# A two-layer diffusion step on one core: other homes for split weights, token-ordered output products, and new step lengths in the planner

## The chip, the cores and the metric

The kernel runs on one core of a Trainium2 chip. The metric is the device time of one execution in microseconds, from start to end on that core; smaller is better. A core has five engines that run side by side, each its own stream of instructions in order: TensorE (PE; its weight loads are shown apart as PEld), VectorE (DVE), ScalarE (ACT), GpSimd (POOL) and SyncE (SP), which here only issues DMA transfers.

## The reference: what is computed

One inference step of a two-layer backbone, for one prompt of 128 tokens and 256 latent tokens (384 tokens, three tiles of 128), model width 1024. Every number is fp32. The core of a layer, cut from the reference:

```python
sh1, sc1, g1, sh2, sc2, g2 = jnp.split(mod, 6, axis=-1)      # mod = silu(c) @ w_mod + b_mod
h = rmsnorm(x, p['norm1_g']) * (1 + sc1) + sh1
proj = h @ p['w_in']
q_r, f_f, f_b, i_r, g_r, q_a, k_a, v_a = jnp.split(proj, ...)
...
o_r = o_f + o_b[:, ::-1]                                     # 4 recurrent heads, both directions
o_r = rmsnorm(o_r, p['hgrn_norm_g']).reshape(B, T, W_R) * jax.nn.silu(g_r)
...
o_a = attend_blocks(qa, k_all, v_all)                        # 8 query heads on 2 key heads
x = x + g1 * (jnp.concatenate([o_r, o_a], axis=-1) @ p['w_out'])
h2 = rmsnorm(x, p['norm2_g']) * (1 + sc2) + sh2
x = x + g2 * (jnp.square(jax.nn.relu(h2 @ p['w1'])) @ p['w2'])
```

After two layers comes a last rmsnorm with a gain. Outputs are both token groups' results, the prompt's new keys and values of each layer, and the final states of the recurrent scan.

## The kernel before

**Split weights.** Matmuls run on operands of a reduced fp32 format, so each fp32 operand is split into a hi half and a lo half, and each product is three matmuls added up in one PSUM bank: hi·hi, lo·hi, hi·lo. A weight block (128 x 1024, or 128 x 768 for the query and key rows) is loaded by SP into one of four `raw` buffers; ACT copies it to the hi half (`hi_chain`, L403); DVE subtracts to the lo half (`lo_chain`, L411), which frees the raw buffer. A half is freed by the last matmul that reads it. There are four ordinary `hi` and four ordinary `lo` buffers. Some blocks are marked in a table `extra` with a class of their own and take their halves from memory that is idle at that time: in before, class "C" (a third of the MLP weights, in region C) and class "U" (see below).

**Regions.** Three large areas of SBUF have several lives. A and B (5376 columns each) hold the recurrent scan's data of one pair of heads each, and afterwards the MLP: columns 0 to 3071 hold the hi (A, `mA`) and lo (B, `mB`) halves of the MLP's input, and columns from 3072 on the halves of its activations. C holds token data and later "C" weights. `Hh` and `Hl` (8 blocks of 384 columns) hold the halves of the normalised layer input; when the input projection is done, blocks 0 to 3 take the recurrent heads' outputs.

**A layer.** Normalise the input and transpose it (L521 square, L524 scale and bias of the mean, L537 scale, L542 transposes, L554/556 modulation, L565/566 split). Query/key rows, eight blocks `qk` k = 0 to 7, three tiles, each with a 512-column (L618) and a 256-column matmul (L619). Feature tiles of the scan (L637). Chunks i and g, the values and gates (L596). Between these stand attention (L824, L846, L892) and the scan of the two pairs of heads: levels (L991), the two 64-level pieces (L977), state (L1060, L1066), then for each pair of heads and token tile the head output, three matmuls (L1089, L1092, L1093). Its way on is a chain over four engines: ACT squares (L1101), DVE (L512) and POOL (L514, a power) make the reciprocal root, DVE scales and gates (L1108, which reads the gate product of that tile), PE transposes (L1113), ACT (L1117) and DVE (L1118) split the result into `Hh` and `Hl`. Then the output projection, 48 steps of three matmuls (L668): step (j, t, hf) multiplies tile t by half hf of the columns of weight block j; j = 0 to 3 are the attention blocks `outA`, j = 4 to 7 the recurrent ones `outR` 0 to 3, where 4 and 5 need the first pair of heads and 6 and 7 the second. DVE updates x (L696 times the gate row G, L698 add). Norm again, then the MLP: first product (L1179, with L1194 for its head part), activation (ACT L1164/1166, DVE L1167), second product (L1205), x update. After the second layer: gain multiply (DVE L1267), norm, scale (L1255/1257), output DMA (L1261). Modulation weights are multiplied by c either on PE (L458, two rows of output only) or on DVE (L427), between other work.

**What sets the order.** The order of instructions is made when the program is built, by a list scheduler (`Sched`). The work is written as chains that yield steps: engine, estimated length, what it reads and writes, which buffers it takes and gives back, and for PE a kind (d dense products; t transposes, m and f other small matmuls) and a `hold`. The scheduler keeps a clock per engine, works out when each chain's next step could start, and picks the one with the smallest value, adjusted by priority; what it picks is emitted, and every engine gets its instructions in that order. So a longer estimate for one step moves others. For PE the value is worked out in `start_of`:

```python
sw = self.SWITCH.get((self.kind, kind), 0.0)
v = max(s + hold, free) if self.kind == "d" else max(s, free) + (STAY if kind == "d" else 0.0)
```

`s` is when its data are there, `free` when PE is. After a dense step, a small one is valued as if its data came `hold` (1 or 2 us) later; after a small step, in before, another small one counts from the moment its data are there, and a dense one 0.15 later.

**Names and lines that the change touches.** `units` is the order in which weights are loaded; `wcls` gives a block's class; `hi_chain` waits for the region of a class to be ready; `win_chain`, `wout_chain` are the products of the input and output projection; `mlp_reg` hands out regions A and B for the MLP; `hg_reg` hands them to the scan; `mlp_chain` is the MLP on PE; `final_gain` is L1267.

## Time and profile before

| | |
|---|---|
| median of 3 runs | 988.65 us |
| lowest, highest | 988.31, 991.17 us |
| the profiled execution | 988.47 us |
| its span | 986.7 us |
| mean granted TensorE clock | 0.998 |
| busy: PE / PE weight load | 98% / 85% |
| busy: DVE / ACT / POOL | 69% / 51% / 4% |
| HBM over the span | 166 GB/s |

The span runs from the first to the last instruction that the profiler recorded; the profiled execution took 1.77 us more than its span. A busy share is that of the whole span. In lists of waits, a line such as "PE bank L1113 <- DVE t L1108: 1.4, 6, 0.4" says that PE, at line 1113, writing a PSUM bank, was idle for what DVE wrote at line 1108: 1.4 us in total, in 6 places, 0.4 the longest. A line of the timeline gives the start in us, the duration, engine, line, operation, output and inputs, the matmul's size, output shape, how many were put together (x8), and in brackets the idle time just before with what ended it. Buffer numbers are left out of names: `t` is one of eight scratch tiles, `bank` one of eight PSUM banks, `cst` the constants with the identity, `sm` small statistics.

### The profile page before, as it was taken

Reading aid. Unit: us, or ns where it says so; the run is one execution under the profiler, and the core shown is the slowest. Engines: PE = TensorE matmul, PEld = TensorE weight load, DVE = VectorE, ACT = ScalarE, POOL = GpSimd, SP = SyncE. Lnnn points to the kernel's source line nnn. Section 1 sums busy time; section 2 is a strip of 40 time slices with the busy share of each in tenths; the row PEclk is TensorE's granted clock in tenths of the full one; section 3 lists DMA queues with packets and bytes.
Section 4 is the critical chain, followed back from the end, with each engine's and each line's share of the span. In section 5 each row is a group of like instructions: output and inputs, shape, how many; then the busy total and the mean of one; then the engine's idle time right before and its main releaser. Section 6 shows DMA issues by size and latency. Waiting matters only on the chain.

```text
span 986.7 us, 17386 instructions
## 1 busy us (share of the span) xinstructions
PE 971.8 (98%) x6935; PEld 837.2 (85%) x6937; DVE 684.9 (69%) x1180; ACT 499.7 (51%) x913; POOL 36.0 (4%) x37
## 2 busy tenths in 40 slices
PE   8999999999999999999999999999999999999997
PEld 5796788878989889889888879787899999999895
DVE  3688777777788989989575979967765444444436
ACT  4467564546543444444445686645664444444332
POOL 0020000010000000000001100011100000000000
PEclk9999999999999999999999999999999999999999
DMA  9968676252677787877525322433336444544511
GB/s 312 305 181 253 196 223 189 59 167 88 207 231 249 246 256 236 242 252 233 173 74 144 105 68 87 110 95 112 113 117 217 147 124 149 147 148 149 192 44 64
DMA packets 140801, 165.39 MB, mean 168 GB/s; under 512 B 5889, under 2 KB 105889, under 8 KB 140209
## 3 DMA queue, kind: packets, MB, share of 16 engines
q1 hardware_dynamic: 140720, 164.29, 54.4%
q8 instruction: 54, 0.88, 0.4%
q14 instruction: 27, 0.21, 0.1%
HBM read 161.35 MB, written 2.92 MB: 166 GB/s over the span
## 4 chain that ended last, share of the span: by engine, by line
PE 90%; DMA 4%; DVE 3%; issue 1%; ACT 1%; POOL 1%; SPq 0%; POOLq 0%; ACTq 0%; DVEq 0%
PE bank L1179 26%; PE bank L1205 26%; PE bank L637 9%; PE bank L596 6%; PE bank L668 6%; PE bank L618 3%; PE bank L619 1%; PE bank L892 1%; PE bank L458 1%; PE bank L991 1%; PE bank L846 1%; PE bank L1194 1%; DMA eB<-w_mod_d 1%; PE bank L824 1%; PE bank L542 1%
## 5 line engine op out<-in xcount | busy, mean ns | idle before, releaser
L403 ACT CAST hi<-raw 128x1024 fp32r<-128x1024 f32 (+1 forms) x152 | 155.7, 1029 | 117.5 <-DMA raw<-w_d 45.3
L411 DVE TENSOR_TENSOR lo<-raw,hi 128x1024 fp32r<-128x1024 f32 (+1 forms) x152 | 179.5, 1192 | 50.7 <-ACT hi L403 50.2
L427 DVE SCALAR_TENSOR_TENSOR t<-raw,cT,t 128x512 f32<-128x512 f32 x196 | 135.2, 745 | 8.6 <-DMA raw<-w_mod_d 8.4
L1179 PE MATMUL bank<-mA,hi 128*128 128x384 f32 (+1 forms) x336 | 111.5, 332 | 0.0
L1179 PE MATMUL bank<-mA,lo 128*128 128x384 f32 (+1 forms) x336 | 111.1, 331 | 0.0
L1179 PE MATMUL bank<-mB,hi 128*128 128x384 f32 (+1 forms) x336 | 110.9, 330 | 0.0
L1167 DVE TENSOR_TENSOR mB<-t,mA 128x384 fp32r<-128x384 f32 x64 | 35.7, 557 | 102.7 <-ACT mA L1166 102.5
L1164 ACT ACTIVATE t<-bank 128x384 f32<-128x384 f32 x64 | 31.4, 491 | 140.1 <-PE bank L1179 140.0
L1205 PE MATMUL bank<-lo,mA 128*128 128x512 f32 (+1 forms) x255 | 99.3, 389 | 0.0
L1205 PE MATMUL bank<-hi,mB 128*128 128x512 f32 (+1 forms) x255 | 99.2, 389 | 0.0
L1205 PE MATMUL bank<-hi,mA 128*128 128x512 f32 (+1 forms) x255 | 99.0, 388 | 0.0
L1179 PE MATMUL bank<-mA,wts 128*128 128x384 f32 (+1 forms) x352 | 89.4, 327 | 0.0
L1205 PE MATMUL bank<-wts,mA 128*128 128x512 f32 (+1 forms) x268 | 87.8, 389 | 0.0
L403 ACT CAST wts<-raw 128x1024 fp32r<-128x1024 f32 x44 | 46.2, 1050 | 50.5 <-DMA raw<-w_d 27.2
L411 DVE TENSOR_TENSOR wts<-raw,wts 128x1024 fp32r<-128x1024 f32 x44 | 53.6, 1222 | 21.6 <-ACT wts L403 21.4
L637 PE MATMUL bank<-Hh,hi 128*128 128x384 f32 x192 | 67.7, 352 | 0.0
L1179 PEld LDWEIGHTS bank<-mA,hi 128*128 128x128 f32 x336 | 63.2, 188 | 1.9 <-issue 0.4
L637 PE MATMUL bank<-Hh,lo 128*128 128x384 f32 x192 | 64.6, 336 | 0.0
L637 PE MATMUL bank<-Hl,hi 128*128 128x384 f32 x192 | 64.4, 335 | 0.0
L1179 PEld LDWEIGHTS bank<-mB,hi 128*128 128x128 f32 x336 | 63.2, 188 | 1.4
L1179 PEld LDWEIGHTS bank<-mA,wts 128*128 128x128 f32 x352 | 62.6, 188 | 1.7 <-issue 0.9
L1179 PEld LDWEIGHTS bank<-mA,lo 128*128 128x128 f32 x336 | 63.2, 188 | 0.0
(251 smaller groups left out, 1947.2 us busy)
## 6 DMA issues: line engine op xcount, KB each, us to landing
raw<-w_d SPq DMA_DIRECT2D x128, 512.0 KB, 4.4
raw<-w_mod_d SPq DMA_DIRECT2D x80, 512.0 KB, 3.8
raw<-w_in_d SPq DMA_DIRECT2D x40, 512.0 KB, 4.5
raw<-w_in_d SPq DMA_DIRECT2D x16, 384.0 KB, 6.2
G<-grow SPq DMA_DIRECT2D x4, 1024.0 KB, 5.9
raw<-w_out_d SPq DMA_DIRECT2D x16, 256.0 KB, 3.9
raw<-w_out_d SPq DMA_DIRECT2D x8, 512.0 KB
eB<-w_mod_d SPq DMA_DIRECT2D x12, 256.0 KB, 5.3
```

What stands on the lines that cost most here:

```text
L403: yield S("ACT", c_act(n), lambda u=u, n=n: ACT.copy(out=get(("hi",) + u)[:, 0:n], in_=get(("raw",) + u)[:, 0:n]), r=[("rawk",) + u] + ([( ...
L411: yield S("DVE", c_dve(n), lambda u=u, n=n: V.tensor_tensor(out=get(("lo",) + u)[:, 0:n], in0=get(("raw",) + u)[:, 0:n], in1=get(("hi",) + ...
L427: V.scalar_tensor_tensor(out=o, in0=raw, scalar=c, in1=o, op0=ALU.mult, op1=ALU.add)
L458: PE.matmul(get(nm)[32 * j:32 * j + m, 0:N], cT[:, k, 0:m], raw[:, o:o + N], start=k == 0, stop=k == 7, tile_position=(0, 32 * j))
L596: PE.matmul(ps, a, b, start=(first and k == 0 and i == 0), stop=(last and k == kk - 1 and i == 2))
L618: PE.matmul(get(aq), a, b[:, 0:512], start=st and i == 0, stop=sp and i == 2)
L637: PE.matmul(ps, a, b, start=(k == 0 and i == 0), stop=(k == 7 and i == 2))
L668: PE.matmul(ps, a, b, start=j == 0 and i == 0, stop=j == 7 and i == 2)
L1164: yield S("ACT", c_act(384, True), lambda: ACT.activation(out=get(r_)[:, 0:384], in_=get(z)[:, 0:384], func=AF.Relu), r=[z], acq=[("t2", r ...
L1167: yield S("DVE", c_dve(384), lambda: V.tensor_tensor(out=get(u)[1], in0=get(t_)[:, 0:384], in1=get(u)[0].bitcast(F32), op=ALU.subtract), r ...
L1179: PE.matmul(get(z)[:, cs], a, b, start=(k == 0 and i == 0), stop=(k == 7 and i == 2))
L1205: PE.matmul(get(bank)[:, c0 % 512:c0 % 512 + c1 - c0], a, b, start=(f == f0 and i == 0), stop=(f == NF - 1 and i == 2))
```

## The change

**Homes of split weights.** Of the output projection's recurrent blocks, `outR` 2 and 3 had the class "U" before: columns 3072 to 5119 of regions A and B, ready when both pairs of heads are done. Now `outR` 0 has class "H", the upper four blocks of `Hh` and `Hl`, ready when the last product of the input projection is issued; `outR` 1 has class "A", columns 3072 to 5119 of region A, ready when the first pair of heads is done; 2 and 3 take ordinary buffers. `mlp_reg` hands out A and B in two steps for this. Of the second layer's query/key blocks, k = 0 to 2 have a new class "Q": columns 0 to 3071 of regions A (hi) and B (lo), ready after the last first product of the MLP of layer 0 (`qfree`). The scan of layer 1 then also waits for the last query/key product before it takes the regions.

**Order of the output projection.** The first two weight blocks, j = 0 and 1, are now taken tile by tile (t, hf, j) where before all tiles were done with one block (j, t, hf). The other six were by tiles already.

**The slack rule.** After a small step, another small one is now valued as if its data came up to `SLACK` = 0.5 us later.

**Step lengths.** Ten estimated lengths on DVE and ACT are made longer (by 0.1 to 0.6 us); one line stands for them below. `final_gain` has a later priority (3.0 for 2.125).

```diff
+QN = 3
+SLACK = 0.5
+FG_P = 3.0
...
-        v = max(s + hold, free) if self.kind == "d" else max(s, free) + (STAY if kind == "d" else 0.0)
+        v = max(s + hold, free) if self.kind == "d" else max(s, free) + STAY if kind == "d" else max(s + min(hold, SLACK), free)
...
-        yield S("DVE", 0.6, lb3, r=["lb2"], w=["lb"])
+        yield S("DVE", 1.2, lb3, r=["lb2"], w=["lb"])
...
-                    r=[("rawk",) + u] + ([({"C": "wtsreg", "U": "mlpreg"}[extra[u]], u[0])] if u in extra else []), ...
+                    r=[("rawk",) + u] + ([({"C": "wtsreg", "A": "mlpregA", "H": "hfree", "Q": "qfree"}[extra[u]], u[0])] if u in extra else []), ...
...
-        yield S("PE", 0.0, lambda: None, w=[("win_done", l)])
+        def hfree():
+            for c, t in (("hiH", Hh), ("loH", Hl)):
+                sch.add_slots((c, l), [t[:, 4:8].rearrange("p a b -> p (a b)")[:, 0:1024]])
+        yield S("PE", 0.0, hfree, w=[("win_done", l), ("hfree", l)])
...
-        for j in range(8 - WOT):
-            for t in range(NT):
-                for hf in range(2):
+        for t in range(NT):
+            for hf in range(2):
+                for j in range(8 - WOT):
                     yield step(j, t, hf, (t, hf) == (2, 1))
...
-                r=(["early_done"] if hp else []) if l == 0 else [("mlp_done", l - 1)], w=[("hgreg", l, hp)])
+                r=(["early_done"] if hp else []) if l == 0 else [("mlp_done", l - 1), ("acc", l, "qa", NT - 1, "done")], w=[("hgreg", l, hp)])
...
+        def f0():
+            a = region("A", f"mA{l}", F32R)
+            sch.add_slots(("hiA", l), [a[:, 3072:4096]])
+            sch.add_slots(("loA", l), [a[:, 4096:5120]])
+            mreg[l] = [a]
...
-            for c, r in (("hiU", a), ("loU", b)):
-                sch.add_slots((c, l), [r[:, 3072 + i * 1024:4096 + i * 1024] for i in range(2)])
...
-        yield S("POOL", 0.0, f, acq=[("rA", ("rmA", l)), ("rB", ("rmB", l))], r=[("ot", l, 0), ("ot", l, 1)], w=[("mlpreg", l)])
+        yield S("POOL", 0.0, f0, acq=[("rA", ("rmA", l))], r=[("ot", l, 0)], w=[("mlpregA", l)])
+        yield S("POOL", 0.0, f, acq=[("rB", ("rmB", l))], r=[("ot", l, 0), ("ot", l, 1)], w=[("mlpreg", l)])
...
+        def qfree():
+            for c, r in zip(("hiQ", "loQ"), mreg[l]):
+                sch.add_slots((c, l + 1), [r[:, i * 1024:(i + 1) * 1024] for i in range(QN)])
+        yield S("PE", 0.0, qfree, w=[("qfree", l + 1)])
...
+            extra.update({(l, "qk", k): "Q" for k in range(QN)})
...
-        extra.update({(l, "outR", h): "U" for h in range(8 - WOT, 4)})
+        extra.update({(l, "outR", 0): "H", (l, "outR", 1): "A"})
...
-            sch.spawn(final_gain(t), 2.125)
+            sch.spawn(final_gain(t), FG_P)
```

The changed program has up to 15 lines more: L411 is L414 there, L524 is L527, L537 is L540, L596 is L599, L668 is L674, L696/698 are L702/704, L1089/1092/1093 are L1095/1098/1099, L1113 is L1119, L1267 is L1282.

**DVE at the boundary of the layers.** The rows are DVE's, from the x updates at the end of the first layer's MLP (L696, L698; `x_92` to `x_94` are the three tiles) to the second layer's norm; `lo` buffers filled from `raw` with 768 columns are the second layer's query/key rows. Before, around the first two of these lo halves:

```order
L537 TENSOR_SCALAR t_6_113<-x_93,sm 128x512
L537 TENSOR_SCALAR t_7_114<-x_93,sm 128x512
L698 TENSOR_TENSOR x_94<-x_94,t_3_110 128x512
L554 TENSOR_SCALAR t_0_107<-bank_63,modA_82,modS_86 128x128 x4
L411 TENSOR_TENSOR lo_124<-raw_117,hi_120 128x768
L696 TENSOR_TENSOR t_5_112<-bank_65,G 128x512
L566 TENSOR_TENSOR Hl<-t_4_111,Hh 128x4x128
L566 TENSOR_TENSOR Hl<-t_0_107,Hh 128x4x128
L698 TENSOR_TENSOR x_94<-x_94,t_5_112 128x512
L411 TENSOR_TENSOR lo_125<-raw_115,hi_121 128x768
```

And now:

```order
L414 TENSOR_TENSOR mB_2274<-raw_115,mA_2272 128x768
L702 TENSOR_TENSOR t_1_108<-bank_67,G 128x512
L704 TENSOR_TENSOR x_92<-x_92,t_1_108 128x512
L414 TENSOR_TENSOR mB_2274<-raw_117,mA_2272 128x768
L414 TENSOR_TENSOR mB_2274<-raw_118,mA_2272 128x768
L702 TENSOR_TENSOR t_4_111<-bank_61,G 128x512
L704 TENSOR_TENSOR x_92<-x_92,t_4_111 128x512
L414 TENSOR_TENSOR lo_123<-raw_116,hi_119 128x768
L527 TENSOR_SCALAR sm<-sm 128x1
```

The lo halves of k = 0 to 2 are made in region B (`mB`), around the first tile's x updates and ahead of its norm; that of k = 3 follows in an ordinary buffer. Before, they came behind the second tile's norm, among the third tile's x updates.

**PE at the head outputs of the first layer.** The rows are PE's, from the head outputs of the second pair of heads (three matmuls each; `hg` is the scan's region, `tok` the token data, `S_103` a state) on; two transposes with `cst` are one head pair's output on its way back, L668 (L674) is the output projection, L599 the gate chunk. Before:

```order
L1089 MATMUL bank_68<-tok_539,hg_538 128x128
L1092 MATMUL bank_68<-hg_538 128x128
L1093 MATMUL bank_68<-S_103,hg_538 128x128
L1113 MATMUL bank_62<-cst,t_1_108 128x128 x2
L668 MATMUL bank_61<-hi_119,mAh 128x512
L668 MATMUL bank_61<-hi_119,mAl 128x512
L668 MATMUL bank_61<-lo_123,mAh 128x512
L668 MATMUL bank_64<-hi_119,mAh 128x512
```

And now:

```order
L1095 MATMUL bank_61<-tok_539,hg_538 128x128
L1098 MATMUL bank_61<-hg_538 128x128
L1099 MATMUL bank_61<-S_103,hg_538 128x128
L1119 MATMUL bank_64<-cst,t_6_113 128x128 x2
L599 MATMUL bank_63<-hi_122,Hh 128x512
L599 MATMUL bank_63<-hi_122,Hl 128x512
L599 MATMUL bank_63<-lo_126,Hh 128x512
L599 MATMUL bank_63<-hi_122,Hh 128x512
L599 MATMUL bank_63<-hi_122,Hl 128x512
L599 MATMUL bank_63<-lo_126,Hh 128x512
L1119 MATMUL bank_65<-cst,t_3_110 128x128 x2
L1119 MATMUL bank_67<-cst,t_5_112 128x128 x2
```

The last six products of the gate chunk come behind the head outputs, between two pairs of transposes; before, the gate chunk was done by then, and the output projection's first products followed the transposes.

**DVE at the end.** The rows are DVE's last x updates of the third tile, in quarters (256 columns), with the gain multiply (L1267, in the change L1282) and the first step of the last norm (L524, L527). Before:

```order
L696 TENSOR_TENSOR t_0_107<-bank_66,G 128x256
L1267 TENSOR_TENSOR t_5_112<-x_94,S_103 128x256
L524 TENSOR_SCALAR sm<-sm 128x1
L698 TENSOR_TENSOR x_94<-x_94,t_0_107 128x256
L696 TENSOR_TENSOR t_7_114<-bank_68,G 128x256
L698 TENSOR_TENSOR x_94<-x_94,t_7_114 128x256
L1267 TENSOR_TENSOR t_3_110<-x_94,S_103 128x256
L524 TENSOR_SCALAR sm<-sm 128x1
```

And now:

```order
L702 TENSOR_TENSOR t_0_107<-bank_63,G 128x256
L704 TENSOR_TENSOR x_94<-x_94,t_0_107 128x256
L527 TENSOR_SCALAR sm<-sm 128x1
L702 TENSOR_TENSOR t_7_114<-bank_64,G 128x256
L704 TENSOR_TENSOR x_94<-x_94,t_7_114 128x256
L1282 TENSOR_TENSOR t_5_112<-x_94,S_103 128x256
L1282 TENSOR_TENSOR t_4_111<-x_94,S_103 128x256
L527 TENSOR_SCALAR sm<-sm 128x1
```

The gain multiply that stood between the last two x updates now stands behind both.

More of the change, by code (lines that the diff above doesn't have):

```diff
@@ L262, in ini @@
             V.memset(sel[:, 33:34], 1.0)
-        yield S("DVE", 1.0, ini, w=["ini"])
+        yield S("DVE", 1.25, ini, w=["ini"])
         yield S("ACT", 1.5, lambda: ACT.activation(out=sg, in_=smalls[:, 0:16], func=AF.Sigmoid), r=["smalls"], w=["sg"])
@@ L840, in nrm @@
                 V.tensor_scalar(out=get(pp[kv]), in0=get(pp[kv]), scalar1=mx[:, 4 + kv:5 + kv], scalar2=None, op0=ALU.mult)
-        yield S("DVE", 0.08 + 2 * c_dve(384, True, 1), nrm, r=[nm + (2,)], w=[nm + (3,)])
+        yield S("DVE", 0.2 + 2 * c_dve(384, True, 1), nrm, r=[nm + (2,)], w=[nm + (3,)])
         def tr():
@@ L876, in nrm @@
             V.tensor_tensor(out=v3(get(pp), 4), in0=v3(get(pp), 4), in1=bc(mx[:, 8:12], 128), op=ALU.mult)
-        yield S("DVE", 0.1 + c_dve(512), nrm, r=[pp], w=[pp + (2,)])
+        yield S("DVE", 0.2 + c_dve(512), nrm, r=[pp], w=[pp + (2,)])
         def tr():
@@ L961, in pr @@
             V.tensor_tensor(out=PR[:, cs], in0=PR[:, cs], in1=get(tk)[:, 0:384], op=ALU.mult)
-        yield S("DVE", 2 * c_dve(384), pr, r=[("hgs3", l, h, d) for d in range(2)] if l else [], acq=[("t2", tk)], rel=[tk], w=[("hgi", l, h)])
+        yield S("DVE", 1.05, pr, r=[("hgs3", l, h, d) for d in range(2)] if l else [], acq=[("t2", tk)], rel=[tk], w=[("hgi", l, h)])
     def hg_levels(l, hp):
@@ L1043, in pl32 @@
                 ACT.copy(out=at(j, 32, 32 * (j ^ 1)), in_=v3(get(("hgp", l, hp, 6))[32 * j:32 * j + 32, 0:192], 6))
-        yield S("ACT", 4 * c_act(192, True), pl32, r=[("hgp", l, hp, 7)], rel=[("hgp", l, hp, 6)], w=[("AT", l, hp, 1)])
+        yield S("ACT", 1.15, pl32, r=[("hgp", l, hp, 7)], rel=[("hgp", l, hp, 6)], w=[("AT", l, hp, 1)])
         def pl():
@@ L1048, in pl @@
                 V.tensor_copy(out=at(j, 32, 32 * j), in_=AC[32 * j:32 * j + 32])
-        yield S("DVE", 4 * c_dve(192, True), pl, r=[("hgp", l, hp, 7), ("AC", l, hp)], w=[("AT", l, hp, 2)])
+        yield S("DVE", 0.95, pl, r=[("hgp", l, hp, 7), ("AC", l, hp)], w=[("AT", l, hp, 2)])
     def hg_state(l, h):
@@ L1132, in f @@
             V.tensor_tensor(out=v3(gSs[l][t], 4), in0=v3(gSs[l][t], 4), in1=hg.unsqueeze(1).to_broadcast([128, 4, 128]), op=ALU.mult)
-        yield S("DVE", 2 * c_dve(512), f, r=[("gs", l, t), "consts"], rel=[ag], w=[("gS", l, t)])
+        yield S("DVE", 1.32, f, r=[("gs", l, t), "consts"], rel=[ag], w=[("gS", l, t)])
     mreg = {}
```

10 lines of the change are left out of this document (4 added, 6 removed).

## The prediction

> **What bounds the kernel now.** I read the page first, then the list of TensorE's waits, then the busy time by stage, and last the rows around each wait. On the page: the span, TensorE's busy line and its row of the slices.
>
> ```profile
> span 986.7 us, 17386 instructions
> PE 971.8 (98%) x6935; PEld 837.2 (85%) x6937; DVE 684.9 (69%) x1180; ACT 499.7 (51%) x913; POOL 36.0 (4%) x37
> PE    8999999999999999999999999999999999999997
> ```
>
> PE (TensorE) is busy in 971.8 of 986.7 us; 14.9 us are all that any order of the work can win without removing a matmul, and this change removes none: by the order of instructions both programs issue 5805 matmuls, line by line the same counts. Only the first and the last slice are under nine tenths. So the question is how much of the small idle time in between goes. TensorE's waits, with total, count and longest:
>
> ```profile
> PE bank L311 <- DVE sel L260: 2.1, 1, 2.1
> PE bank L1113 <- DVE t L1108: 1.4, 6, 0.4
> PE bank L458 <- DMA raw<-w_mod_d: 0.7, 1, 0.7
> PE bank L618 <- DVE lo L411: 0.7, 1, 0.7
> PE bank L542 <- DVE t L537: 0.6, 2, 0.4
> PE bank L977 <- ACT hg L1006: 0.5, 1, 0.5
> PE bank L458 <- DMA eB<-w_mod_d: 0.4, 1, 0.4
> PE bank L458 <- DMA eC<-w_mod_d: 0.3, 1, 0.3
> PE bank L458 <- issue: 0.3, 1, 0.3
> ```
>
> They sum to 7.0 us. 2.1 is the first instruction, 1.0 the last three lines (the start), and 3.9 lies in places that the change reorders: six waits at the transposes of the head outputs (L1113), one at a modulation weight (L458), one at the next layer's first rows (L618), part of L542's, and one at the 64-level of the scan (L977). Where nothing waits the stream is full; by stage, with us, then busy us of PE, weight load, DVE, ACT and POOL, then clock:
>
> ```profile
> 190.00:207.00 17.00, 16.29 (x99) 13.09 (x98) 14.06 (x37) 9.26 (x30) 3.83 (x3) 1.00 0.24 69
> 250.00:500.00 250.00, 250.00 (x1339) 222.75 (x1338) 210.04 (x297) 111.55 (x165) 0.00 (x0) 1.00 0.72 227
> ```
>
> The first stage holds three of the L1113 waits; the second is the first layer's MLP, 250 us without a gap, which the change leaves word for word as it was.
>
> **What a wait costs.** The gap in the list understates it, since a broken stream must refill. The third L1113 wait and the products around it:
>
> ```profile
> 205.01 0.40 PE L668 MATMUL bank<-lo,mAh 128*128 128x512 f32 x1
> 205.56 0.44 PE L1113 MATMUL bank<-cst,t 128*128 128x128 f32 x2 [0.15 <-DVE t L1108]
> 205.75 0.48 PE L668 MATMUL bank<-hi,mAh 128*128 128x512 f32 x1
> 206.06 0.40 PE L668 MATMUL bank<-hi,mAl 128*128 128x512 f32 x1
> 206.30 0.40 PE L668 MATMUL bank<-lo,mAh 128*128 128x512 f32 x1
> ```
>
> A product of L668 is followed after 0.24 us (206.06 to 206.30) when nothing waits. Here 0.55 pass (205.01 to 205.56), so the wait cost 0.31, 0.16 more than its gap of 0.15. I add 0.16 to every gap. The same rows price a detour: the first product after the transposes takes 0.31 (205.75 to 206.06), 0.07 more than its 0.24.
>
> **Part 1, the next layer's first rows.** Their hi and lo halves for k 0 to 2 move to the regions that hold the MLP's input, free after the last product of L1179. Before, PE and DVE at that place:
>
> ```profile
> 497.61 0.69 DVE L696 TENSOR_TENSOR t<-bank,G 128x512 f32<-128x512 f32 x1 [1.98 <-PE bank L1205]
> 513.44 0.28 PE L619 MATMUL bank<-hi,Hl 128*128 128x256 f32 x1
> 513.55 0.40 PE L618 MATMUL bank<-lo,Hh 128*128 128x512 f32 x1
> 515.54 0.95 DVE L411 TENSOR_TENSOR lo<-raw,hi 128x768 fp32r<-128x768 f32 x1
> 515.56 0.28 PE L619 MATMUL bank<-hi,Hl 128*128 128x256 f32 x1
> 516.55 0.51 PE L618 MATMUL bank<-lo,Hh 128*128 128x512 f32 x1 [0.71 <-DVE lo L411]
> 517.95 0.28 PE L619 MATMUL bank<-lo,Hh 128*128 128x256 f32 x1
> 518.48 1.09 PE L542 MATMUL bank<-cst,t 128*128 128x128 f32 x8 [0.25 <-DVE t L537]
> ```
>
> The lo half of k 2 is made at 515.54, when PE already wants it: 0.99 us pass instead of 0.11 (513.44 to 513.55), a cost of 0.88. At 517.95 PE goes on to the third tile's transposes and waits again: 0.25 and 0.16, so 0.41. After the change three of these halves stand among the first tile's x updates, where DVE has idle time (1.98 us at 497.61 alone, against three times 0.95), and 30 products instead of 24 stand ahead of the transposes. Gain 1.29. The cover is thin for the third lo, which now stands ahead of the first tile's norm: if all 0.95 of it were late there, 0.3 would be left. Bounds 0.3 to 1.3; I take 1.2. Past the second layer's entry nothing else moves: the scan's region now also waits for the last of those products, but its first user stands behind them on PE anyway, so that costs nothing. On SP two row loads go ahead of the gate row load, whose reader is the out projection; nothing there.
>
> **Part 2, output weights, token order and the slack rule.** L1113 has six waits, 1.4 us of gaps and six times 0.16: 2.4. The order puts 6 to 18 products (0.24 each, 1.4 to 4.3 us) between a head output and its transposes, where before the twelve small products or none stood. What the cover has to hide is the chain over ACT, DVE and POOL; POOL's step in it takes 0.70, or 1.60 when a lo half runs beside it:
>
> ```profile
> 199.03 0.70 POOL L514 TENSOR_TENSOR sm<-sm,pw 128x2 f32<-128x2 f32 x1 [22.78 <-DVE sm L512]
> 200.53 1.60 POOL L514 TENSOR_TENSOR sm<-sm,pw 128x2 f32<-128x2 f32 x1 [0.80 <-DVE sm L512]
> 200.17 0.59 PE L1113 MATMUL bank<-cst,t 128*128 128x128 f32 x2 [0.35 <-DVE t L1108]
> ```
>
> So I leave one wait of the longest size (0.35 and 0.16) in one layer: gain 1.9, bounds 0.5 and 2.4. The same rule, that a small step after a small step needs half a microsecond of slack, takes L977 from behind L991 to behind 21 dense products: gain 0.5 + 0.16 = 0.66, and spreads the three modulation groups at 141 us to pairs with 6 and 9 products ahead: gain 0.7 + 0.16 = 0.86, bounds 0 (the loads move with the products that free their buffers) and 0.86; I take 0.6. The output weights' other homes (the upper half of Hh and Hl, region A) free buffers no one waited for in the list above; the price is that the last two now wait for an ordinary buffer until the first 36 products are done. Their two casts and subtractions have eight steps of three products, 24 x 0.24 = 5.8 us; that hides them, so zero, and up to 1 us if DVE is late.
>
> What the new order adds: counted in it, TensorE passes from dense to small work 104 times instead of 95, and between kinds of small work 46 times instead of 54. At 0.07 each the nine cost 0.6, the eight save as much or less: I take 0.35, bounds 0 and 0.6.
>
> Every other place of both attention and scan stretches is reordered too, and none of it can be seen in the trace of before: waits of the sizes in the list may appear. Three new ones of 0.16 + 0.1 would be 0.8; bounds 0 and, as many as there are now, 3.9. I take 0.8.
>
> **Part 3, the start.** Loads set the pace there. The order moves groups of modulation weights ahead of row products:
>
> ```profile
> 31.10 0.62 PE L458 MATMUL bank<-eC,cT 128*2 128x128 f32 x16
> 31.54 0.62 PE L458 MATMUL bank<-xnT,cT 128*2 128x128 f32 x16
> 32.97 0.96 DVE L411 TENSOR_TENSOR lo<-raw,hi 128x768 fp32r<-128x768 f32 x1 [2.14 <-ACT hi L403]
> ```
>
> The xnT group moves ahead of six products, and the products that need the lo half of 32.97 come before one more group instead of after it. If that half lands as before, a group of up to 0.62 is left to do behind it. The three start waits (1.0) may shrink in exchange. Bounds 1.0 gained and 0.6 lost; I take 0.5 lost, nearest the rows of the group.
>
> **Part 4, the end.** The gain multiply of 256 columns (L1267) goes behind the last x update:
>
> ```profile
> 979.09 0.28 PE L1205 MATMUL bank<-lo,mA 128*128 128x256 f32 x1
> 979.15 0.42 DVE L1267 TENSOR_TENSOR t<-x,S 128x256 f32<-128x256 f32 x1
> 979.67 0.42 DVE L698 TENSOR_TENSOR x<-x,t 128x256 f32<-128x256 f32 x1
> 980.45 0.42 DVE L698 TENSOR_TENSOR x<-x,t 128x256 f32<-128x256 f32 x1
> 980.97 0.42 ACT L521 ACTIVATE t<-x 128x256 bf16<-128x256 f32 x1 [1.47 <-DVE x L698]
> 981.51 0.21 DVE L524 TENSOR_SCALAR sm<-sm 128x1 f32<-128x1 f32 x1 [0.18 <-ACT t L521]
> ```
>
> PE is done at 979.37; DVE is the end's bound. The multiply gives back some 0.4 in front of the last update, and two of them then run beside ACT's square (0.54 from 980.97 to 981.51, room for one and a bit). Gain 0.3, bounds 0 and 0.4.
>
> **The sum.** 1.2 + 1.9 + 0.66 + 0.6 + 0.3 = 4.66, less 0.35 and 0.5, is 3.8 gained. The unseen waits take the rest: 3.8 - 0.8 = 3.0. But the step lengths also come closer to the trace (a scan's copies, sums and the first memsets are longer in the plan), which speaks for few new ones, so I count half of them, 0.4, and get 3.4. The profiled execution took 988.47 (its span and 1.77 around it), 0.18 below the median of 988.65: 988.47 - 3.4 = 985.1.
>
> The Trainium skill, "Perfetto Trace Analysis", section "Identifying the Most-Contended Engine", holds matmul busy time to be a bad measure of headroom and wants the share of weight loading instead. By that, 986.7 - 837.2 = 149.5 us would be open, and the sum could be many times as large. The trace disagrees for this kernel: 250 us without one wait show 222.75 of weight load, 89%, so 85% over the span is nearly full.
>
> **The rivals.** *Waits move, they don't go.* Layer 0's last transposes now wait for the last tile's gate product as well, and the start loses its 0.6. Then Part 2 gives 0.5 + 0.66 and Part 1 its 1.2, Part 4 0.3, less 0.35, 0.6 and 0.4: 1.3 gained, 987.2. For it speaks DVE, busy 14.06 of 17 us in that stage; against it that every wait in the list is under a microsecond and the new cover is above one.
>
> *The filler runs out (slower).* Layer 1 now spends 63 products before the last head output's transposes, 24 before; only the first 60 of the 144, as they stand, need no output of the second pair of heads. From the 61st on, each microsecond by which the scan's chain is late is a microsecond of PE. Three POOL steps at 1.60 for 0.70 and two lo halves (0.95 or more) ahead in DVE's queue are 2.7 + 1.9 = 4.6 late; with the 1.2 (half of 2.4) that one layer's L1113 waits should give, 985.1 + 5.8 = 990.9 in one layer, 996.7 in both. It decides from 2.2 us of lateness on (3.4 less 1.2). Against it: half a microsecond of slack is now asked for, and the longer step lengths make the plan less hopeful.
>
> *Nothing to measure.* The modulation wait stays, the start loses 0.6 and new waits take 3: 988.6.
>
> *The clock.* In a stream cut into more pieces the granted clock could fall; in the stage from 190 to 207, the most cut one, it is 1.00. If it fell to half in that stage and its twin in layer 1, 2 x 16.29 would be added: 1017.7. The Trainium skill, "Perfetto Trace Analysis", section "Matmul Optimizations", asks for matmuls back to back in batches since the engine scales its power by use; by that rule the nine more cuts speak against the change. The trace shows no such drop at the cuts there are.
>
> **How the numbers follow.** A change of less than 0.3% (3 us) can't be told from none when this kernel is measured. Forecast (gains of 3 to 5.5 us): 0.55, faster. Waits move, with the weaker half of the forecast's own spread: 0.28, within 0.3%. Nothing to measure: 0.09, within. Filler: 0.07, of it 0.06 slower and 0.01 within. Clock: 0.01, slower. That makes 0.55 faster, 0.38 within and 0.07 slower. The range: all gains at their upper bounds (1.3 + 2.4 + 0.66 + 0.86 + 0.4 + 1.0 = 6.6) give 981.9; the low end is 982.3. Above, the range takes in waits that move and most of the nothing case: 988.6. It leaves out the filler, the clock and half of the nothing case, with 0.05 below.
>
> **What would show it.** Right: in the changed kernel's list of waits no L618 on lo L411, no L977, at most two of L1113 and a total under 5 us; at the end the last square of ACT some 0.4 us closer behind PE's last matmul. Wrong: a new line of 1 us or more on the out projection's products or on L1113, L596 or L637; the first row product of the long block at the start later than before; or a granted clock under 0.99.

## The result and the profile after

The changed kernel takes 982.06 us (median of 6 runs, 981.62 to 982.52), the kernel before 989.16 beside it (6 runs, 987.77 to 991.17): a ratio of 0.9926, with a 95% interval of 0.9913 to 0.9939, so 6 to 8.6 us less. The forecast was 985.1 with a range of 982.3 to 988.6: the direction was right, the gain was about twice as large, and the time lies just under the range. The two profiled executions differ by 6.2 us, 988.47 against 982.29; all that follows is worked out from them.

From the page after, the span, the busy line and TensorE's row of the slices; PE is busy for 3.5 us less with the same matmuls, and idle for 12.2 us instead of 14.9:

```profile
span 980.5 us, 17364 instructions
PE 968.3 (99%) x6936; PEld 837.0 (85%) x6937; DVE 683.0 (70%) x1180; ACT 499.2 (51%) x913; POOL 33.6 (3%) x37
PE    8999999999999999999999999999999999999997
```

TensorE's waits after, in the same columns as those of before. They sum to 4.9 us; those on the lo half of the second layer's rows and on the 64-level are gone, and of the six on the head transposes (now L1119) one is left:

```profile
PE bank L314 <- DVE sel L263: 2.1, 1, 2.1
PE bank L461 <- DMA raw<-w_mod_d: 0.5, 1, 0.5
PE bank L1119 <- DVE t L1114: 0.5, 1, 0.5
PE bank L621 <- ACT Hh L581: 0.4, 1, 0.4
PE bank L472 <- ACT t L468: 0.4, 2, 0.2
PE bank L461 <- DMA eB<-w_mod_d: 0.3, 1, 0.3
PE bank L792 <- DVE t L786: 0.3, 1, 0.3
PE bank L545 <- DVE t L540: 0.2, 1, 0.2
PE bank L314 <- issue: 0.2, 1, 0.2
```

So the list is 2.1 us shorter and the span 6.2. To see where the rest went I cut the program at places that both orders share: the last row product of a layer's query/key rows (L619, L622) and the last product of its out projection (L668, L674). Between two such rows the same products run, in whatever order. The four rows of after, from its timeline:

```profile
51.81 0.28 PE L622 MATMUL bank<-lo,Hh 128*128 128x256 f32 x1
...
232.94 0.39 PE L674 MATMUL bank<-lo,Hh 128*128 128x512 f32 x1
...
537.21 0.28 PE L622 MATMUL bank<-lo,Hh 128*128 128x256 f32 x1
...
704.17 0.39 PE L674 MATMUL bank<-lo,Hh 128*128 128x512 f32 x1
```

And of before:

```profile
51.72 0.28 PE L619 MATMUL bank<-lo,Hh 128*128 128x256 f32 x1
...
234.85 0.39 PE L668 MATMUL bank<-mB,Hh 128*128 128x512 f32 x1
...
540.62 0.28 PE L619 MATMUL bank<-lo,Hh 128*128 128x256 f32 x1
...
710.07 0.39 PE L668 MATMUL bank<-mB,Hh 128*128 128x512 f32 x1
```

The lengths between them, here and for all kernels below: **start** (to the first row), **layer 0** (to the second), **rows** (the second layer's 144 row products with what stands between them, from the first product to the third row above), **layer 1** (to the fourth). Both MLPs are as long after as before.

| kernel (profiled execution) | start | layer 0 | rows | layer 1 | median us |
|---|---|---|---|---|---|
| before | 51.7 | 183.1 | 27.76 | 169.45 | 989.2 |
| after | 51.8 | 181.1 | 26.27 | 166.96 | 982.1 |
| after again | 53.3 | 180.1 | 26.61 | 166.99 | 983.1 |
| no_plan | 52.2 | 182.7 | 26.61 | 168.76 | 986.3 |
| no_slack | 53.1 | 181.3 | 26.62 | 169.04 | 986.2 |
| no_lengths | 53.4 | 181.1 | 26.62 | 167.12 | 985.2 |
| no_q | 53.4 | 180.2 | 27.74 | 166.96 | 983.8 |
| q_only | 53.2 | 183.7 | 26.62 | 169.28 | 988.3 |
| plan_only | 53.7 | 181.1 | 27.74 | 173.84 | 992.4 |
| no_homes | 51.8 | 181.4 | 26.61 | 173.68 | 989.9 |
| no_class | 52.1 | 180.7 | 26.62 | 166.26 | 981.7 |
| no_tiles | 54.2 | 181.1 | 26.59 | 167.77 | 985.1 |
| homes_only | 53.2 | 183.1 | 27.75 | 168.82 | 988.1 |
| old_start | 51.8 | 178.8 | 26.26 | 166.97 | 981.2 |
| best | 52.9 | 179.3 | 26.26 | 166.18 | 980.6 |

The last two stretches hardly depend on the execution: four kernels with one order of layer 1 (after, after again, no_q, old_start) read 166.96, 166.99, 166.96 and 166.97. The start does: between 51.6 and 54.2 in the profiles of all kernels, and 51.8 and 53.3 in two executions of the changed kernel itself. So the first two columns are good to a microsecond or two, the last two to some tenths. At the end, from PE's last matmul to the span's end, 7.33 us before have become 7.05.

**Where the unlisted part went.** The head transposes are the clearest place. Four of them in the first layer, with the product ahead; before (the timeline, start and length in us), and after:

```profile
193.82 1.17 PE L1066 MATMUL bank<-tok,t 128*128 128x128 f32 x9
194.95 1.10 PE L1113 MATMUL bank<-cst,t 128*128 128x128 f32 x4
195.89 0.61 PE L1089 MATMUL bank<-tok,hg 128*128 128x128 f32 x4
```

```profile
197.37 0.39 PE L599 MATMUL bank<-lo,Hh 128*128 128x512 f32 x1
197.60 0.60 PE L1119 MATMUL bank<-cst,t 128*128 128x128 f32 x4
197.95 0.48 PE L674 MATMUL bank<-hi,mAh 128*128 128x512 f32 x1
```

Before, TensorE's list has no wait at the four, and yet they take 1.10 us instead of 0.60: they start 0.26 us apart, where after the six dense products they start 0.11 apart. The weight loads of the four (PEld) and the VectorE multiplications that write their inputs (L1108, L1114) show why; before, and after:

```profile
194.54 1.13 DVE L1108 SCALAR_TENSOR_TENSOR t<-bank,sm,tok 128x128 f32<-128x128 f32 x4
194.95 0.91 PEld L1113 LDWEIGHTS bank<-cst,t 128*128 128x128 f32 x4 [0.15 <-DVE t L1108]
```

```profile
196.06 1.32 DVE L1114 SCALAR_TENSOR_TENSOR t<-bank,sm,tok 128x128 f32<-128x128 f32 x4
197.37 0.59 PEld L1119 LDWEIGHTS bank<-cst,t 128*128 128x128 f32 x4
```

Each transpose reads a multiplication of its own. Before, these run 0.26 us apart at that very moment, and each transpose starts 0.05 us after its own one ends (the last at 195.72, after 195.67). After, all four multiplications are done at 197.38, before the first transpose starts at 197.60. So the slow steps are waits for VectorE; the first of them stands in the line of the weight loads (0.15). Small work ahead is not the reason: two transposes directly behind head outputs, at 195.99 in the profile after, also start 0.11 us apart.

TensorE's list misses these waits because a matmul's record is longer than the usual step to the next one, 0.27 us against 0.11 here and 0.40 against 0.24 for a product of L668. A wait shorter than this difference of 0.16 us leaves no idle time, and TensorE counts as busy in it. The groups of instructions by line, in the stretch of the first layer's out projection (total, then mean ns of one; before, then after), show the waiting transposes as longer matmuls:

```profile
L1113 PE MATMUL bank<-cst,t 128*128 128x128 f32 x12 | 2.9, 310 | 0.7 <-DVE t L1108 0.7
```

```profile
L1119 PE MATMUL bank<-cst,t 128*128 128x128 f32 x12 | 2.0, 272 | 0.0
```

The Trainium skill, "TensorE: Matmul & The Clock Gate", section "Architectural detail: the array is 16× 32×32, not 1× 128×128", says that TensorE's queue can pull weight loads ahead of matmuls that still run. The rows agree with that: after, the first load starts at 197.37, 0.23 us ahead of its matmul and beside the last product, while before, where the data are late, the first load starts together with its matmul at 194.95. No run here looks into the queue itself.

### The profile page after: what moved, and what is told of

Same layout as the page of the kernel before. It is cut to its first block, busy times and chain, and to the rows that moved or that the text cites. A ratio compares the mean times of both kernels' runs of the same rounds, so it can differ in the third digit from the quotient of the medians.

```text
span 980.5 us, 17364 instructions
## 1 busy us (share of the span) xinstructions
PE 968.3 (99%) x6936; PEld 837.0 (85%) x6937; DVE 683.0 (70%) x1180; ACT 499.2 (51%) x913; POOL 33.6 (3%) x37
## 4 chain that ended last, share of the span: by engine, by line
PE 90%; DMA 5%; DVE 2%; issue 1%; POOL 1%; SPq 0%; ACT 0%; POOLq 0%; ACTq 0%; DVEq 0%
PE bank L1189 26%; PE bank L1215 26%; PE bank L640 10%; PE bank L599 7%; PE bank L674 6%; PE bank L997 2%; PE bank L621 1%; PE bank L898 1%; DMA raw<-w_in_d 1%; PE bank L1204 1%; PE bank L852 1%; PE bank L461 1%; PE bank L830 1%; PE bank L545 1%; DMA eB<-w_mod_d 1%
## 5 line engine op out<-in xcount | busy, mean ns | idle before, releaser
L414 DVE TENSOR_TENSOR lo<-raw,hi 128x1024 fp32r<-128x1024 f32 (+1 forms) x149 | 176.7, 1198 | 52.3 <-ACT hi L406 50.5
L406 ACT CAST hi<-raw 128x1024 fp32r<-128x1024 f32 (+1 forms) x149 | 153.0, 1033 | 103.7 <-DMA raw<-w_d 44.1
L414 DVE TENSOR_TENSOR wts<-raw,wts 128x1024 fp32r<-128x1024 f32 x44 | 53.6, 1223 | 24.3 <-ACT wts L406 24.2
```

The lines of the kernel that those rows point to most:

```text
L406: yield S("ACT", c_act(n), lambda u=u, n=n: ACT.copy(out=get(("hi",) + u)[:, 0:n], in_=get(("raw",) + u)[:, 0:n]), r=[("rawk",) + u] + ([( ...
L414: yield S("DVE", c_dve(n), lambda u=u, n=n: V.tensor_tensor(out=get(("lo",) + u)[:, 0:n], in0=get(("raw",) + u)[:, 0:n], in1=get(("hi",) + ...
```

## The experiments

**The planner's rules.** The first question was which part holds the gain of the two layers: the planner's two rules (theory A) or the out weights' homes with the tile order (theory B).

no_plan: the ten old step lengths and the old rule, all else as in the change.

```diff
-        yield S("DVE", 1.25, ini, w=["ini"])
+        yield S("DVE", 1.0, ini, w=["ini"])
...
-SLACK = 0.5
+SLACK = 0.0
```

> All of the change but the longer step lengths and the slack rule. By theory A (the planner's two rules hold the gain of both attention and scan stretches, 4.5 us in the traces; the out weights' homes and the tile order hold none) the run gives 4.5 back: 986.5, a span near 985, and the list of TensorE's waits has the six on the head transposes (1.4) and the one on the 64-level (0.5) again. By theory B (the homes and the tile order give the cover for the transposes) about half comes back, 984.3, with at most two waits on the transposes.

986.32 (985.65 to 989.43), ratio to before 0.9967 (0.9950 to 0.9983). The total is theory A's, the list is not: in layer 1 two waits are there, not four.

```profile
PE bank L1119 <- DVE t L1114: 0.5, 1, 0.5
PE bank L983 <- ACT hg L1012: 0.5, 1, 0.5
```

Layer 1 keeps 0.69 of its 2.49 us, so the homes hold something too. The two rules apart:

no_slack (`SLACK = 0.0` alone):

> The change with SLACK = 0, so the old rule with the longer lengths. In its order the second layer's 64-level stands right behind the scan levels again and most head transposes behind head outputs. Theory A1 (the rule is what matters, lengths alone do little): 4 us back, 986. Theory A2 (either of the two gives most of it): 1 to 1.5 us back, 983.3, of it 0.66 the wait on the 64-level.

no_lengths (the ten old lengths alone):

> The change with the old step lengths, with the slack rule. Theory A1 (the rule matters): 982.5. Theory A2 (either gives most): 983. If the lengths are what makes the plan right, waits appear where the plan is too hopeful, on the transposes above all, and 985 or more.

986.16 (985.45 to 986.40) and 985.22 (983.34 to 986.29). Layer 1, the column that can be read, says A1: without the rule it is 2.1 us longer (169.04), without the lengths 0.16 (167.12). The total of no_lengths is higher than this explains and lies where the third expectation put it, but the waits on the transposes that this one named are not in its list. Its start in the trace is 1.6 us later than in the profile after, with the same order there but for one of the warming matmuls, and whether the rest is the start's spread stays open.

**The next layer's first rows.** no_q takes the class "Q" away, q_only gives it alone to the kernel before:

```diff
-            extra.update({(l, "qk", k): "Q" for k in range(QN)})
```

> The change with the second layer's first rows in ordinary buffers, as before; everything else of its order is the same. Theory A: 1.5 us back (the stretch of the rows took 1.49 less in the trace after), 983.6, with the wait of 0.7 on the lo half and the two on the third tile's transposes. Rival: the better plan ahead of it makes the lo half early anyway, 982.1.

> The kernel before with the next layer's first rows in the MLP's idle columns, nothing else. 1.1 to 1.5 us less than before in the stretch of the rows, so a ratio of 0.9985 and no wait on the lo half; the rest of the trace as before.

983.79 (982.45 to 985.28), and 988.33 (986.22 to 989.47) with a ratio of 0.9986 (0.9977 to 0.9996). No_q has the wait on the lo half again, as long as before:

```profile
PE bank L621 <- DVE lo L414: 0.7, 1, 0.7
```

The stretch of the rows is 27.74 to 27.76 in each of the four kernels without "Q" and 26.26 to 26.62 in each with it. This part adds 1.1 to 1.5 us whatever else is in the kernel.

**The out weights' homes and the tile order.** no_homes undoes both (class "U" for `outR` 2 and 3, the loops j, t, hf), plan_only is the kernel before with the two planner rules:

```diff
-            extra.update({(l, "outR", 0): "H", (l, "outR", 1): "A"})
+            extra.update({(l, "outR", h): "U" for h in range(8 - WOT, 4)})
...
-        for t in range(NT):
-            for hf in range(2):
-                for j in range(8 - WOT):
+        for j in range(8 - WOT):
+            for t in range(NT):
+                for hf in range(2):
```

> The change with the out weights' old homes and the old order of their first two blocks. Theory A: 982.1 to 982.4, the stretches of both layers as long as after. Theory B: 983.3, and new waits on the head transposes or on the out projection's lo halves.

> The kernel before with the longer step lengths and the slack rule alone. Theory A (these hold 4.5 us of both layers' stretches, the homes none): 984, that is after plus 1.5 for the rows and 0.3 for the end. Theory B (homes and tile order hold half of the transposes' part; the run without the plan still gained 0.5 and 0.7 in the two layers): 985, with one or two more waits on the transposes.

989.89 (989.42 to 991.25) and 992.43 (991.85 to 993.16), the second slower than before by a ratio of 1.0036 (1.0023 to 1.0048). Both theories fell: the planner's rules without the homes lose all that they win and more, and all of it in layer 1, which is 4.2 and 4.4 us longer than before and 6.7 and 6.9 longer than after. The place, in the timeline of no_homes (L1116 is its L1113, L671 its L668):

```profile
683.82 0.38 PE L1116 MATMUL bank<-cst,t 128*128 128x128 f32 x2
686.06 0.73 PE L1116 MATMUL bank<-cst,t 128*128 128x128 f32 x2 [1.86 <-DVE t L1111]
688.20 0.80 PE L671 MATMUL bank<-mA,Hh 128*128 128x512 f32 x1 [1.41 <-ACT mA L406]
```

TensorE waits 1.86 us for the last head output, and then 1.41 for the cast of `outR` 2 into region A (`mA`), which is free only when that head output is through. No other product is left. The busy times in that place, in steps of 4 us (PE, weight load, DVE, ACT, POOL, then the granted clock, DMA share and GB/s):

```profile
680.00:684.00 4.00, 4.00 (x27) 3.48 (x25) 1.71 (x6) 0.69 (x4) 0.70 (x1) 1.00 0.26 91
684.00:688.00 4.00, 0.94 (x4) 0.32 (x2) 1.63 (x5) 2.05 (x7) 0.70 (x1) 0.79 0.00 0
688.00:692.00 4.00, 3.76 (x8) 2.58 (x9) 3.50 (x3) 2.99 (x4) 0.00 (x0) 0.50 0.33 96
692.00:696.00 4.00, 4.00 (x16) 3.23 (x16) 3.08 (x5) 1.03 (x3) 0.00 (x0) 0.86 0.92 277
```

The stalls are 3.3 us. The granted clock falls to 0.50 between the two and stays there for 6.8 us, in which a product takes 0.43 us instead of 0.23 from start to start, so the loss doubles.

This gave theory C: what an old home costs depends on how many products stand between the last head transposes, which open it, and the first product that reads it. Counted in the orders of layer 1: 36 before, 0 in no_homes and plan_only. The new homes open earlier; there the same count (to the first product that reads one) is 15 after. Three more kernels split the part:

no_class has the old homes with the new tile order (12 products), no_tiles the new homes with the old order of the first two blocks (6), homes_only puts both into the kernel before (24).

> The change with the out weights' old homes alone; the first two blocks stay in tile order. Theory C (what the old homes cost under the new plan is set by how many products stand between the last head transposes, which open them, and the first product that reads them): 36 in the kernel before and no stall there, 0 in the run without homes and tile order and 3.3 us of stalls in the second layer, 12 here (2.9 us): between the two, under 1.5 us of stalls there, the granted clock 1.00, and 982.5 to 985. If it is not their number but the homes as such, 988 or more with the granted clock under 0.9 again.

> The change with the first two weight blocks in their old order; the homes are new. Theory C: the new homes open long before, so no stall: 982 to 983.3. If the tile order is what keeps the filler, stalls of 1 us or more on the head transposes of the second layer and 985 or more.

> The kernel before with the new homes and the tile order, without planner rules and without the rows' homes. Theory C: nothing stalled on the old homes there (36 products of cover), so within 0.1% of before; the run without the plan suggests 0.5 to 1.2 us less, with two waits on the head transposes instead of six: ratio 0.998 to 1.0.

981.74 (980.86 to 981.82), ratio 0.9917 (0.9903 to 0.9930); 985.07 (983.56 to 985.89), ratio 0.9952 (0.9939 to 0.9966); 988.13 (986.22 to 989.98), ratio 0.9985 (0.9975 to 0.9995). With 12 products the old homes cost nothing: layer 1 is even 0.7 shorter than after. That is the direction of theory C, but the total lies 0.8 under its range: 12 products of cover were enough. So the new homes are not needed where the tile order is, and no_tiles shows that the new homes without the tile order avoid the stalls of no_homes too. No_tiles missed its expectation by 1.8 us. In layer 1 it is 0.8 longer than after, by a wait of the out projection for the last head output:

```profile
PE bank L674 <- DVE t L1114: 0.8, 1, 0.8
```

The other 2 us of its total stand in the start by its profile (54.2), although its orders there are those of the change; why five of its six times lie above all of the change's I can't say.

**Stalls and the clock.** The three stall kernels are the change with n copies in place on VectorE (n = 3, 7, 13) between two products of the second layer's MLP, and no other instruction moved:

```diff
+                def stall():
+                    uh = get(("us", l, 12))[0]
+                    V.tensor_copy(out=scr, in_=zb[0][:, 0:1])
+                    for _ in range(3):
+                        V.tensor_copy(out=uh, in_=uh.bitcast(F32))
```

> The change with one stall of TensorE set into the full stream of the second layer's MLP: 3 copies in place of 128x384 on VectorE between two products; no other instruction moves. About 1.2 us idle. Theory K1 (a stall costs its gap and 0.1 to 0.3 to refill, whatever its length): the stretch grows by 1.3 to 1.5 us. Theory K2 (past some length the granted clock falls): the same here, clock 1.00.

> The same with 7 copies, about 2.4 us idle. K1: 2.5 to 2.7 us more. K2: the same, or up to 2 us on top and a granted clock under 1 in the 4 us behind it, if the bound lies under 2.4.

> The same with 13 copies, about 4 us idle. K1: 4.1 to 4.3 us more, clock 1.00 behind the stall. K2: 6 to 8 us more, with a granted clock near 0.5 for 4 to 8 us behind the stall, as in the run without homes where stalls of 1.86 and 1.41 us stood close together.

The copies took longer than I had estimated: the stalls are 1.83, 3.41 and 5.78 us. From the product ahead of the stall to the 80th behind it pass 18.31, 21.42 and 24.30 us. The changed kernel needs 16.09 there, and 16.22 with the tile of 4 bytes that these kernels have too (shift_4, below). Against the latter the cost is 2.1, 5.2 and 8.1, so 0.3, 1.8 and 2.3 over the stall itself. The rows of the windows that hold the stall and what follows it, for 3 copies, for 7 and for 13 (columns as above):

```profile
832.00:836.00 4.00, 2.17 (x10) 1.79 (x10) 3.34 (x8) 2.48 (x4) 0.00 (x0) 1.00 0.32 97
836.00:840.00 4.00, 4.00 (x21) 3.54 (x21) 2.87 (x4) 1.05 (x1) 0.00 (x0) 1.00 0.47 127
```

```profile
832.00:836.00 4.00, 0.59 (x2) 0.50 (x2) 3.16 (x9) 2.47 (x4) 0.00 (x0) 0.94 0.32 96
836.00:840.00 4.00, 4.00 (x13) 3.15 (x12) 3.68 (x6) 0.00 (x0) 0.00 (x0) 0.64 0.18 24
```

```profile
833.00:837.00 4.00, 1.43 (x3) 1.16 (x4) 3.79 (x10) 0.00 (x0) 0.00 (x0) 0.54 0.02 4
837.00:841.00 4.00, 4.00 (x13) 3.12 (x11) 2.77 (x4) 0.00 (x0) 0.00 (x0) 0.61 0.30 72
841.00:845.00 4.00, 4.00 (x23) 3.82 (x22) 1.23 (x1) 1.05 (x1) 0.00 (x0) 1.00 0.59 190
```

Theory K2 holds for these three: 1.83 us leave the clock at 1.00, 3.41 and 5.78 us bring it down, and 3.4 and 4.5 us after their end it is full again. The Trainium skill, "TensorE: Matmul & The Clock Gate", section "What's actually happening", puts the fall to half rate at an idle window of about 3.4 us. The two longer stalls agree: the fall comes 3.4 and 3.5 us after they begin. But so long a stall is not needed. In no_homes the clock falls 0.25 us behind the first stall, which is of 1.86 us, and ahead of the second, which begins at 686.8. A wait of the same 1.86 us at the start of no_tiles (18.95 to 20.81) leaves it at 1.00. The rows, of no_homes and of no_tiles (the granted clock is the third number from the right):

```profile
684.00:686.30 2.30, 0.44 (x3) 0.14 (x1) 1.20 (x4) 0.89 (x5) 0.70 (x1) 1.00 0.00 0
686.30:686.80 0.50, 0.50 (x2) 0.18 (x1) 0.00 (x0) 0.00 (x0) 0.00 (x0) 0.51 0.00 0
```

```profile
18.90:20.80 1.90, 0.05 (x1) 0.00 (x0) 0.17 (x1) 0.99 (x2) 0.00 (x0) 1.00 1.02 335
20.80:24.20 3.40, 3.39 (x33) 2.41 (x37) 2.31 (x7) 0.51 (x1) 0.00 (x0) 1.00 1.09 366
```

So the length of a stall alone does not decide. In each of these traces the changes of the granted clock lie 3.41 us or a multiple of it apart (835.50 and 838.91 in stall_7, 833.30 and 840.12 in stall_13, 686.31 and 693.13 in no_homes). Counted on in such steps, an estimate, the stall of no_homes lies in one step whole, while that of no_tiles falls into two with 1.3 and 0.5 us, and that of stall_3 into two with 0.4 and 1.4. How much of one step is idle would tell them apart, but no run was made to test this.

The totals were too high for these costs: 990.43 (988.58 to 992.07) for 3 copies, 994.08 in one run for 7, 995.43 (994.67 to 996.85) for 13. The first layer's MLP, where nothing stalls, took 257.3 to 257.6 us in them, from its first to its last product of L1179, and 255.3 in the change. The kernels have one more tile in SBUF, 4 bytes a partition, ahead of the regions. Two kernels with such a tile and no stall:

```diff
+    scr = sb("scr", [128, 1])
+    V.memset(scr, 0.0)
```

> The change with one more tile of 4 bytes per partition in SBUF, allocated ahead of the three regions, and one memset of it at the start; no other instruction differs and there is no stall. In the stall runs, which have that tile too, the first layer's MLP, where nothing stalls, took 257.3 to 257.6 us for 255.3. If the shift of the regions by 4 bytes is the cause, both MLPs are 2 to 2.5 us longer here and the run takes 986.5 to 987.5; if not, 982.

> The same with a tile of 64 bytes per partition. If what matters is that the regions lie on a boundary of 64 bytes or less, the MLPs take 255.3 us as in the change and the run 982; if any shift does it, or the memset, 986.5 to 987.5.

987.67 (985.96 to 989.19), ratio to before 0.9980 (0.9971 to 0.9990), and 983.71 for 64 bytes (982.86 to 984.29 in three runs; a fourth took 2998 us and is left out), ratio 0.9939 (0.9920 to 0.9959). The MLP of layer 0 takes 257.3 and 255.9 us. The second products of the MLP by line, 250 to 480 us, in the change, with 4 and with 64 bytes:

```profile
L1215 PE MATMUL bank<-hi,mA 128*128 128x512 f32 x102 | 40.0, 392 | 0.0
```

```profile
L1218 PE MATMUL bank<-hi,mA 128*128 128x512 f32 x102 | 40.5, 397 | 0.0
```

```profile
L1218 PE MATMUL bank<-hi,mA 128*128 128x512 f32 x103 | 40.9, 397 | 0.0
```

So the tile of 4 bytes is the cause of the stall kernels' longer MLPs, and not the memset, which the kernel with 64 bytes has too. With 64 bytes these products are as slow, but the first products of that layer make up for most of it (mean step 168.4 ns; 170.2 with 4 bytes, 169.3 in the change). What in the layout does it stays open.

**The start, and both findings together.** old_start applies the slack rule only from 52 us of the plan on; best is old_start with no_class:

```diff
-max(s + min(hold, SLACK), free)
+max(s + min(hold, SLACK if free > 52 else 0.0), free)
```

> The changed kernel once more, beside the runs below on the same chip: 982.1 by the runs so far. The start is what may differ: in two executions with the same order the last product of the first layer's rows came at 51.8 and 53.4 us.

> The change with the slack rule off in the first 52 us of the plan, so that the start has the order of before. If the new order of the start costs what the prediction said (0.5), 981.7; if it costs nothing, 982.3 and the start's end between 51.7 and 53.5 us, where executions of one order lie.

> Two findings put together: the change with the out weights' old homes (first blocks in tile order) and with the slack rule off in the first 52 us of the plan. Each alone was 0.3 to 1 us under the change (981.7 and 981.2). If they add, 980.5 to 981; if their gain was the start's spread between executions, 981.5 to 982.5.

After_again has 983.09 (981.51 to 983.77). Old_start has 981.24 (980.00 to 982.18), ratio 0.9915 (0.9901 to 0.9929), and best 980.56 (979.60 to 981.49), ratio 0.9907 (0.9890 to 0.9923), the lowest of all. Its interval overlaps with that of the change (0.9913 to 0.9939), so by the times alone it is not settled that it is faster; by the trace its layer 1 is 0.78 us shorter (166.18 against 166.96), and old_start and best have the two shortest layers 0, 178.8 and 179.3 against 180.1 to 181.4 with the new start.

## Why the prediction was right in direction and wrong in size

The terms beside what the two profiles show. For the transposes and the modulation it is the time between starts over the usual one, summed over a line's instructions; for the rest the stretches.

| term | predicted | measured |
|---|---|---|
| rows of the next layer | 1.2 | 1.49 (1.1 in most other kernels) |
| head transposes | 1.9 | 3.1 |
| 64-level of the scan | 0.66 | 0.66 |
| modulation groups | 0.6 | 0.7 |
| detours and unseen waits | -0.35 and -0.4 | +0.1 (layer 0 -0.7, layer 1 +0.8) |
| the start | -0.5 | -0.1 |
| the end | 0.3 | 0.28 |
| sum | 3.4 | 6.2 |

- **The list of waits taken as the whole cost** is the step that failed: the gains were priced from TensorE's list alone ("They sum to 7.0 us"). The transposes won 3.1 us where 1.9 was taken, because waits too short for that list were there as well. The bound "14.9 us are all that any order of the work can win without removing a matmul" fails for the same reason: TensorE counts as busy in such waits, and busy time fell by 3.5 us of the 6.2.
- **The rest of the difference.** A loss of 0.75 was put down for the new order, and none came in sum (see "What the order adds"). The start lost 0.4 less than forecast and the rows won 0.3 more. With the 1.2 of the transposes that is nearly all of the 2.8 us between 3.4 and 6.2.
- **The transposes.** Six gaps with 0.16 each (2.4, of which I took 1.9) was the right price for the listed waits: their steps cost 0.36, 0.52 and 0.32 us over the usual in the first layer. The reason given, "since a broken stream must refill", is not what the rows show: 0.16 is the record's length less the usual step, 0.40 - 0.24. The other 0.8 us of a layer, 0.6 of it at the four transposes that VectorE paces, is not in TensorE's list. One listed wait was left in one layer, as forecast.
- **The modulation groups** are right in size only. The wait that was to go is still in this profile, 0.50 us at 147.00 instead of 0.72 at 142.16; in after_again it is gone, and layer 0 is 1.0 us shorter there.
- **What the order adds.** "I take 0.8" for new waits, then half of it, and 0.35 for passages between dense and small work: in layer 0 about that much was lost, in layer 1 as much was won, where attention's products (L846) meet fewer slow steps, by some 0.4 us. I had counted passages, which rose, and not the steps in between. What won the rest in layer 1 stays open.
- **The homes at zero** failed as a step though the number was right for this kernel's sum. "Free buffers no one waited for in the list above" is true of the old order; in the new one the old homes and the old loops together cost 6.7 us in layer 1. The rival "The filler runs out" named the mechanism, at the place and in the layer where it happened, but as a danger of the change; it is a danger of the plan alone. The tile order removes it, and so do the new homes but for a wait of 0.8 us. The clock, a rival with 0.01, came with it, by idle time and not by the number of cuts.
- **The rows, the 64-level and the end** were right in mechanism and size: the waits went, and the last square of ACT starts 1.27 us behind PE's last matmul, before 1.60.

```profile
973.19 0.28 PE L1215 MATMUL bank<-lo,mA 128*128 128x256 f32 x1
...
974.74 0.42 ACT L524 ACTIVATE t<-x 128x256 bf16<-128x256 f32 x1 [1.14 <-DVE x L704]
```

- **The start** at -0.5 may have been right: by the profiles of one execution it is -0.1, by old_start and best against the change and no_class about -1 in the medians, with intervals that overlap. One profile can't tell, since the start moves by up to 2.6 us between executions.
- **The signs.** Every sign named for "right" came: a list of 4.9 us, one wait on the transposes, none on the lo half of L618 or on L977, a closer square at the end. All but the last look at listed waits, and none could tell a gain of 3.4 from one of 6.2.
- **The base.** The forecast went from the profiled 988.47, beside a median of 988.65 in 3 runs; over the runs of all batches the kernel before has medians of 989.2 to 989.9. So the time missed the range by only 0.2 us partly by luck: from 989.16 the forecast would have been 985.8, and its range would have begun at 983.0. The upper end of the range has a slip of its own: the terms of "Nothing to measure" add up to 988.4, not 988.6.

## What to carry to other kernels

On a full TensorE, don't take the list of waits or the idle time for the whole gain: here a wait of up to 0.16 us left TensorE busy by its records. Compare the distance between starts of the same small matmul at different places, and where it is long, look at the engine that writes its input. A memory home or a loop order that no wait points to can still be what allows another order; cost it under the new order, by counting the products between the step that opens the buffer and the first that reads it. And cut both programs at rows that they share before summing anything, so that a start that differs from one execution to the next doesn't hide a stretch that repeats to 0.03 us.

## What the runs showed of the hardware

- Transposes of 128x128 whose data are ready start 0.11 us apart, behind dense and behind small work. Four that each waited for a VectorE multiplication started at its pace, 0.26 us apart, without a line in TensorE's list of waits.
- A matmul's record outlasts the step to the next matmul by 0.16 us (0.40 against 0.24 for 128x512, 0.27 against 0.11 for 128x128).
- A stall of 1.83 us in a full stream cost 2.1 us with the granted clock at 1.00; 3.41 us cost 5.2 and 5.78 us cost 8.1, with the clock at 0.50 for 3.4 and 6.8 us.
- A stall of 1.86 us brought the granted clock to 0.50 in no_homes, and one of the same length left it at 1.00 in no_tiles.
- One tile of 4 bytes a partition ahead of the large buffers made the MLPs' second products about 1% slower (397 ns for 392), each MLP 2 us longer and the kernel some 5 us slower than the change, with a memset as the only instruction more.
